# Summing both halves of a modulation vector over partitions in one group of products

## The chip, the cores and the metric

One core of a Trainium2 chip runs one program. The metric is the device time of one execution in microseconds, as the median over several runs of the same program on the same chip.

## What is computed

Two layers of a conditioned decoder trunk, all in f32, with 256 rows of 1024 columns. Each layer is a feed-forward block, a token mixer and another feed-forward block. Each of the three gets a shift, a scale and a gate, which are nine vectors of 1024 numbers computed from a condition vector `c`:

```python
c_act = jax.nn.silu(c)
for l in range(DEPTH):
    mod = c_act @ w_ada[l] + b_ada[l]
    sh1, sc1, g1, sh2, sc2, g2, sh3, sc3, g3 = jnp.split(mod, N_MOD, axis=-1)
    x = x + 0.5 * g1[:, None, :] * swiglu(modulate(x, sh1, sc1), ffn1_gate[l], ffn1_up[l], ffn1_down[l])
    x = x + g2[:, None, :] * token_mix(modulate(x, sh2, sc2), ...)
    x = x + 0.5 * g3[:, None, :] * swiglu(modulate(x, sh3, sc3), ffn2_gate[l], ffn2_up[l], ffn2_down[l])
return rms_norm(x) * final_norm
```

`modulate` is an RMS norm, times 1 + scale, plus shift. `swiglu(u)` is `(silu(u @ w_gate) * (u @ w_up)) @ w_down` with 2816 hidden columns. What the token mixer does inside does not matter here.

## The kernel before, in words

**Products.** An f32 product is made from three products of a faster format: a weight block is split into a high part (`whi`, a copy by ACT, L177) and a low part (`wlo`, the rest, by DVE, L179), the other operand likewise (`uhi` and `ulo`, or `hh` and `hl` for the hidden tile), and high times high, low times high and high times low are added up in PSUM. One split makes a unit of 128x1024. Weight blocks of 1 MB arrive by DMA from SP's queue in a pool `raws` of four buffers (tile name `raw`), two units to a block. A buffer is free again when its last reader is done, and only then can the DMA of the next block that was given that buffer go out.

**Feed-forward block (`ffn`).** For each of the groups of 256 hidden columns a gate block and an up block are loaded (L625, L626), each gives two units, and `ws_tile` makes 24 products of 256 columns for each unit; `finish_tile` makes the hidden tile from them (`sg` by ACT, `hf32` by DVE, L494, `hh` by ACT, `hl` by DVE, L496). Then the down matrix comes in two column halves (c = 0 and 1), in blocks of four 128-row tiles (L432), two units to a block, twelve products of 512 columns to a unit.

**The modulation vectors (`ada_half`).** They are computed beside this, in pieces: one half of a vector, 512 columns of `w_ada`, is two blocks (L216) of 128x4x512. For each block DVE makes four multiply-and-add instructions into an accumulator `acc` of 128x512 (L222; each takes one of eight columns of `c_act`, `cact`), so that what is left is a sum over the 128 partitions, which `finish` does on PE. A *row channel* (2, 5, 8: the gates) starts from the bias (`binit`), is split by ACT (L229) and DVE (L230) into a high and a low tile, and `finish` sums each with one product of 512 columns against a block of ones, so that the sum stands in every partition. A *column channel* (0, 1, 3, 4, 6, 7: shifts and scales) is wanted with its numbers along the partitions: `column_sums` makes four f32 products of 128 columns whose stationary operand is 32 columns of ones, one for each strip of 32 rows of PSUM; `pick_columns` multiplies by a mask (`mcol`, L194) and reduces (`cs`, L197), and `add_bias` makes the columns (`col`, L203). Channels of layer 0's first block are made otherwise, in `begin`, which uses `pick_columns` too.

All accumulators, of row and of column channels, come from one pool, `keep`, tag `acc`, with two buffers. An accumulator is free again when its products (column) or its two splits (row) are done.

**Order.** `ada_load` takes a list of halves and makes a generator. Each `ada_step`, which `ffn` calls at a group of hidden columns (one or two steps) and at each block of the down matrix (one), brings one w_ada block; a `finish` is issued at the step after its half is complete. The lists are: first feed-forward block of either layer: channels 2, 3, 4, 5, 6 of that layer, two halves each; token mixer of layer 0: channel 7; second feed-forward block of layer 0: channel 8, then 1, 0, 7 of layer 1; token mixer and second block of layer 1: none and channel 8. So ten column vectors go through `ada_half`, in the order 3, 4, 6, 7 of layer 0, and 1, 0, 7, 3, 4, 6 of layer 1. The order of instructions within each engine, and which buffer of a pool a tile gets, are set by a scheduler when the kernel is built, not by hand (save in `begin`).

Of the kernel before, what the change touches and what calls it, by code (L numbers as in the profile page):

```python
# [10 lines left out]
F32 = mybir.dt.float32  # L11
F32R = mybir.dt.float32r
AF = mybir.ActivationFunctionType
ALU = mybir.AluOpType
AX = mybir.AxisListType

P = 128
D = 1024
KD = D // P
# [58 lines left out]
def hybrid_trunk(ctx, tc, t, out):  # L78
    nc = tc.nc
# [7 lines left out]
    keep = ctx.enter_context(tc.tile_pool(name="keep", bufs=1))  # L87
    scr = ctx.enter_context(tc.tile_pool(name="scr", bufs=2))
    small = ctx.enter_context(tc.tile_pool(name="small", bufs=4))
# [14 lines left out]
    def mm(o, a, b, start, stop):  # L104
        last_mm[0] = nc.tensor.matmul(o, a, b, start=start, stop=stop)  # L105
# [7 lines left out]
    ones = const.tile([P, P], F32R, name="ones")  # L113
# [12 lines left out]
    colmask = tab[:, TAB_COL:TAB_COL + 32]  # L126
# [14 lines left out]
    def pool_unit(pool):  # L141
        return (pool.tile([P, 1024], F32R, name="whi", tag="whi"),
                pool.tile([P, 1024], F32R, name="wlo", tag="wlo"))
# [39 lines left out]

    mods = {}

    def column_sums(ps, vec, a, start, stop):

        av = a.rearrange("p (j i r) -> p j i r", j=4, i=4)
        for i in range(4):
            mm(ps[32 * i:32 * i + 32, :P].rearrange("p (j r) -> p j r", j=4), vec, av[:, :, i, :], start, stop)  # L190

    def pick_columns(ps):
        m = small.tile([P, 4, 32], F32, name="mcol", tag="mcol", bufs=1)
        nc.vector.tensor_tensor(m, ps[:, :P].rearrange("p (j r) -> p j r", j=4),  # L194
                                colmask[:, None, :].to_broadcast([P, 4, 32]), ALU.mult)
        cs = small.tile([P, 4], F32, name="cs", tag="cs", bufs=2)
        nc.vector.tensor_reduce(cs, m, AX.X, ALU.add)  # L197
        return cs

    def add_bias(l, ch, n, cs):  # L200
        if (l, ch) not in mods:
            mods[l, ch] = small.tile([P, KD], F32, name="col", tag="col", bufs=8)
        nc.vector.scalar_tensor_tensor(mods[l, ch][:, n * 4:n * 4 + 4], cs, 1.0 if ch in (1, 4, 7) else 0.0,  # L203
                                       bcols[:, l, ch * 8 + n * 4:ch * 8 + n * 4 + 4], ALU.add, ALU.add)

    def ada_half(l, ch, n):
        acc = keep.tile([P, 512], F32, name="acc", tag="acc", bufs=2)
        row = ch in (2, 5, 8)
        n0 = ch * D + n * 512
        wv = t["w_ada"][l].rearrange("(p j) n -> p j n", p=P)  # L210
        if row:
            nc.scalar.dma_start(binit[0:1, :], t["b_ada"][l:l + 1, n0:n0 + 512])
        for j in range(0, KD, 4):
            r = raw_tile()
            rv = r.rearrange("p (j n) -> p j n", j=4)
            nc.sync.dma_start(rv, wv[:, j:j + 4, n0:n0 + 512])  # L216
            for jj in range(4):
                cj = cact[:, j + jj:j + jj + 1]
                if j + jj == 0 and not row:
                    nc.vector.tensor_scalar_mul(acc, rv[:, jj, :], cj)  # L220
                else:
                    nc.vector.scalar_tensor_tensor(acc, rv[:, jj, :], cj, binit if j + jj == 0 else acc,  # L222
                                                   ALU.mult, ALU.add)
            yield
        if row:
            if n == 0:
                mods[l, ch] = keep.tile([P, D], F32, name="g", tag="g", bufs=2)
            hi, lo = (scr.tile([P, 512], F32R, name="acc%d" % i, tag="uf", bufs=2) for i in range(2))
            nc.scalar.activation(hi, acc, AF.Copy)  # L229
            nc.vector.tensor_tensor(lo, acc, hi.bitcast(F32), ALU.subtract)  # L230

            def finish():
                ps = trps()
                mm(ps, ones, hi, True, False)
                mm(ps, ones, lo, False, True)
                nc.scalar.activation(mods[l, ch][:, n * 512:(n + 1) * 512], ps, AF.Copy, scale=1.0 if ch == 5 else 0.5)
        else:
            def finish():
                ps = trps()
                column_sums(ps, ones[:, :32].bitcast(F32), acc, True, True)  # L240
                cs = pick_columns(ps)
                add_bias(l, ch, n, cs)
        ada_late.append(finish)

    ada_late = []
# [211 lines left out]
    def ffn(l, which, uhi, ulo, ada_plan, post, xn=None, side=None):  # L457
# [4 lines left out]
        with tc.tile_pool(name="ffn", bufs=1) as fp, tc.tile_pool(name="fu", bufs=EXTRA) as fu, \  # L462
# [5 lines left out]
            unit_kinds[:] = ["w"] * 4 + ["f"] * EXTRA  # L468
            unit_count[0] = 0
            unit_alloc["f"] = lambda: pool_unit(fu)  # L470
            bank_pools[:] = [psum, fps]
            ada_load(ada_plan)

# [24 lines left out]
            def begin():  # L498
# [7 lines left out]
                ada, gu, more, accs, sums, units = {}, {}, {}, {}, {}, {}  # L506
# [35 lines left out]
                    accs[q] = acc  # L542

                def operands(q):
                    cs = pick_columns(sums[q])
                    for i, ch in enumerate((1, 0)):
                        nc.vector.scalar_tensor_tensor(mods[l, ch][:, q * 2:q * 2 + 2], cs[:, i * 2:i * 2 + 2], float(ch),
                                                       bcols[:, l, ch * 8 + q * 2:ch * 8 + q * 2 + 2], ALU.add, ALU.add)
# [70 lines left out]
            for grp in range(2 if xn is None else 3, KF // 2):  # L619
# [8 lines left out]
                for i in range(2):  # L628
                    f = grp * 2 + i
                    ps = mmps()  # L630
# [13 lines left out]
                xs_gemm(units, ktiles(h[0]), ktiles(h[1]), 512, evac, 6 if c else 0, last if c else None)  # L644
            unit_kinds[:] = ["w"]
            bank_pools[:] = [psum]


    def token_mix(l, uhi, ulo, ada_plan, post):
# [459 lines left out]
    bcols = const.tile([P, DEPTH, 72], F32, name="bcols")  # L1109
# [36 lines left out]
    for hf in range(NH):  # L1146
        r, a, _ = half_rstd(hf)
# [59 lines left out]
```

## Time and profile before

| | |
|---|---|
| median of 3 runs | 1188.9 us (1186.39 to 1190.99) |
| profiled execution | 1184.94 us |
| its span | 1183.1 us |
| mean granted clock of TensorE | 0.995 |
| PE busy | 1151.3 us, 97% of the span |
| DVE busy | 939.1 us, 79% |
| ACT busy | 642.6 us, 54% |

PE is TensorE, DVE VectorE, ACT ScalarE, and SP the engine whose queue issues the weight DMAs. Products are pipelined on PE, so rows of single products overlap, and their distance from start to start is what they cost. Busy shares are means over stages with different limits; the stage that matters here is layer 1's first feed-forward block, whose down products begin at 731 us. L105 is the helper that issues every product, so products are told apart by their tiles: `mm` is a weight product, `tr<-acc,ones` the sum over partitions of an accumulator.

### The profile page before, as it was taken

What the parts mean: (1) busy time and instruction counts of PE and PEld (TensorE: products, weight loads), DVE (VectorE), ACT (ScalarE), POOL (GpSimd) and SP (SyncE); (2) the same over time, 40 slices, a digit from 0 to 9 for tenths busy, and PEclk for the clock granted to TensorE, in tenths of its full rate; (3) what the DMA queues carried; (4) which work ended last, traced back from release to release, by engine and by line L of the source; (5) the groups of instructions that cost most, each with busy time, mean ns of one, the idle gap of its engine ahead of it and who ended that gap; (6) DMA issues with size and microseconds to landing.
All of it is one profiled execution on the core that took longest, in us unless ns stands there. A gap on an engine that the chain in (4) does not pass through costs nothing.

```text
span 1183.1 us, 20211 instructions
## 1 busy us (share of the span) xinstructions
PE 1151.3 (97%) x7886; PEld 1011.7 (86%) x7886; DVE 939.1 (79%) x1889; ACT 642.6 (54%) x1156; POOL 2.2 (0%) x13
## 2 busy tenths in 40 slices
PE   4999999999999999999999999999999999999997
PEld 3799988789977889998879999888997788999985
DVE  4999998778888898798488879975878888865553
ACT  4545444647676564544465444465676756554441
POOL 0000000000000000000000000000000000000000
PEclk8999999999999999999999999999999999999999
DMA  9989999595623579898739979965664264985540
GB/s 331 337 289 342 333 347 364 163 266 168 178 96 104 192 228 306 286 324 311 254 110 312 317 258 349 338 232 146 178 204 117 72 200 133 306 258 189 181 140 36
DMA packets 201970, 274.95 MB, mean 232 GB/s; under 512 B 13613, under 2 KB 119815, under 8 KB 201875
## 3 DMA queue, kind: packets, MB, share of 16 engines
q1 hardware_dynamic: 201119, 273.02, 70.5%
q8 instruction: 62, 1.02, 0.4%
q10 hardware_dynamic: 756, 0.64, 0.2%
q14 instruction: 33, 0.27, 0.1%
HBM read 272.60 MB, written 1.05 MB: 231 GB/s over the span
## 4 chain that ended last, share of the span: by engine, by line
PE 86%; DVE 7%; DMA 3%; ACT 2%; issue 1%; SPq 1%; DVEq 0%; ACTq 0%
PE mm L105 77%; PE tr L108 3%; DMA raw<-in_w_ada 2%; PE sc L105 2%; PE po L105 2%; DVE wlo L179 2%; PE tr L105 2%; ACT whi L177 1%; DVE win L723 1%; DVE acc L222 0%; DVE kd L745 0%; DMA c_in<-in_c 0%; ACT junk L293 0%; DVE acc L541 0%; DVE x L453 0%
## 5 line engine op out<-in xcount | busy, mean ns | idle before, releaser
L179 DVE TENSOR_TENSOR wlo<-raw,whi 128x1024 fp32r<-128x1024 f32 (+5 forms) x400 | 423.0, 1073 | 120.1 <-ACT whi L177 119.3
L177 ACT ACTIVATE whi<-raw 128x1024 fp32r<-128x1024 f32 (+5 forms) x400 | 364.3, 936 | 232.2 <-PE mm L105 103.0
L105 PE MATMUL mm<-uhi,whi 128*128 128x256 f32 x1248 | 348.4, 279 | 0.0
L105 PE MATMUL mm<-uhi,wlo 128*128 128x256 f32 x1248 | 347.1, 278 | 0.0
L105 PE MATMUL mm<-ulo,whi 128*128 128x256 f32 x1248 | 347.1, 278 | 0.0
L105 PEld LDWEIGHTS mm<-ulo,whi 128*128 128x128 f32 x1248 | 236.2, 189 | 0.5
L105 PEld LDWEIGHTS mm<-uhi,whi 128*128 128x128 f32 x1248 | 234.2, 188 | 2.5 <-issue 1.4
L105 PEld LDWEIGHTS mm<-uhi,wlo 128*128 128x128 f32 x1248 | 234.4, 188 | 0.0
L222 DVE SCALAR_TENSOR_TENSOR acc<-raw,cact,acc 128x512 f32<-128x512 f32 x224 | 167.0, 747 | 5.4 <-DMA raw<-in_w_ada 2.4
L105 PE MATMUL mm<-whi,hh 128*128 128x512 f32 x352 | 138.3, 393 | 0.0
L105 PE MATMUL mm<-whi,hl 128*128 128x512 f32 x352 | 137.1, 390 | 0.0
L105 PE MATMUL mm<-wlo,hh 128*128 128x512 f32 x352 | 137.0, 389 | 0.0
L105 PE MATMUL mm<-whi,uhi 128*128 128x512 f32 (+3 forms) x336 | 126.7, 379 | 4.9 <-ACT uhi L554 3.5
L105 PE MATMUL mm<-whi,ulo 128*128 128x512 f32 (+3 forms) x336 | 126.9, 378 | 1.4 <-DVE ulo L342 1.4
L105 PE MATMUL mm<-wlo,uhi 128*128 128x512 f32 (+3 forms) x336 | 125.7, 374 | 0.0
L495 ACT ACTIVATE hh<-hf 128x256 fp32r<-128x256 f32 x70 | 29.1, 416 | 99.3 <-DVE hf L494 99.3
L105 PEld LDWEIGHTS mm<-whi,hh 128*128 128x128 f32 x352 | 66.1, 188 | 15.1 <-issue 1.4
L105 PEld LDWEIGHTS mm<-whi,hl 128*128 128x128 f32 x352 | 66.1, 188 | 13.9
L105 PEld LDWEIGHTS mm<-whi,uhi 128*128 128x128 f32 x336 | 63.5, 190 | 16.8 <-ACT uhi L554 4.1
L105 PEld LDWEIGHTS mm<-wlo,hh 128*128 128x128 f32 x352 | 66.1, 188 | 13.3
L105 PEld LDWEIGHTS mm<-whi,ulo 128*128 128x128 f32 x336 | 63.9, 190 | 12.0 <-DVE ulo L342 3.1
L105 PEld LDWEIGHTS mm<-wlo,uhi 128*128 128x128 f32 x336 | 63.8, 190 | 9.4 <-DVE wlo L179 0.2
(245 smaller groups left out, 1325.3 us busy)
## 6 DMA issues: line engine op xcount, KB each, us to landing
raw<-in_w_ada SPq DMA_DIRECT2D x72, 1024.0 KB, 7.9
raw<-in_ffn_gate SPq DMA_DIRECT2D x41, 1024.0 KB, 7.0
raw<-in_ffn_up SPq DMA_DIRECT2D x41, 1024.0 KB, 6.8
raw<-in_ffn_down SPq DMA_DIRECT2D x40, 1024.0 KB, 7.9
raw<-in_w_in SPq DMA_DIRECT2D x18, 1024.0 KB, 6.8
raw<-in_w_in SPq DMA_DIRECT2D x16, 512.0 KB, 6.2
raw<-in_w_out SPq DMA_DIRECT2D x8, 1024.0 KB, 5.1
raw<-in_ffn_down SPq DMA_DIRECT2D x8, 512.0 KB
```

The source lines that it names most:

```text
L105: last_mm[0] = nc.tensor.matmul(o, a, b, start=start, stop=stop)
L108: nc.tensor.transpose(o, a, ident)
L177: nc.scalar.activation(a, s, AF.Copy)
L179: nc.vector.tensor_tensor(b, s, a.bitcast(F32), ALU.subtract)
L222: nc.vector.scalar_tensor_tensor(acc, rv[:, jj, :], cj, binit if j + jj == 0 else acc, ALU.mult, ALU.add)
L495: nc.scalar.activation(h[0][:, f, :], hf32, AF.Copy)
L723: nc.vector.tensor_tensor(win[i][jj * 64:(jj + 1) * 64, 8 * a:8 * a + 8, g, :], pv[g * 64:(g + 1) * 64, jj, :, a:a + 15], cols[0][jj * 64: ...
```

## The change

The two halves of a column vector are kept in two accumulators (`held`) until the second is complete. Then one `finish` makes 8 products into 128x256 of PSUM, one multiplication, one reduction and one bias for all eight columns. A count of the vectors (`pairs`) sends those with an even number, while a feed-forward block runs, to two accumulators of that block's pool (tag `sgx`, `acc_rooms`); odd ones, and those outside, take the two of `keep`, as row channels do. By that count the vectors of layer 0 are 1 (channel 3, `keep`), 2 (4, `sgx`), 3 (6, `keep`), 4 (7, `keep`, in the token mixer), and those of layer 1 are 5 (1, `keep`), 6 (0, `sgx`), 7 (7, `keep`), 8 (3, `sgx`), 9 (4, `keep`), 10 (6, `sgx`).

```diff
--- before.py
+++ after.py
@@ -183,29 +183,35 @@
 
     mods = {}
 
-    def column_sums(ps, vec, a, start, stop):
-
-        av = a.rearrange("p (j i r) -> p j i r", j=4, i=4)
-        for i in range(4):
-            mm(ps[32 * i:32 * i + 32, :P].rearrange("p (j r) -> p j r", j=4), vec, av[:, :, i, :], start, stop)
-
-    def pick_columns(ps):
-        m = small.tile([P, 4, 32], F32, name="mcol", tag="mcol", bufs=1)
-        nc.vector.tensor_tensor(m, ps[:, :P].rearrange("p (j r) -> p j r", j=4),
-                                colmask[:, None, :].to_broadcast([P, 4, 32]), ALU.mult)
-        cs = small.tile([P, 4], F32, name="cs", tag="cs", bufs=2)
-        nc.vector.tensor_reduce(cs, m, AX.X, ALU.add)
+    def column_sums(ps, vec, halves):
+
+        for n, a in enumerate(halves):
+            av = a.rearrange("p (j i r) -> p j i r", j=4, i=4)
+            for i in range(4):
+                mm(ps[32 * i:32 * i + 32, n * P:(n + 1) * P].rearrange("p (j r) -> p j r", j=4), vec, av[:, :, i, :],
+                   True, True)
+
+    def pick_columns(ps, n):
+        m = small.tile([P, KD, 32], F32, name="mcol", tag="mcol", bufs=1)
+        nc.vector.tensor_tensor(m[:, :n], ps[:, :n * 32].rearrange("p (j r) -> p j r", j=n),
+                                colmask[:, None, :].to_broadcast([P, n, 32]), ALU.mult)
+        cs = small.tile([P, KD], F32, name="cs", tag="cs", bufs=2)
+        nc.vector.tensor_reduce(cs[:, :n], m[:, :n], AX.X, ALU.add)
         return cs
 
-    def add_bias(l, ch, n, cs):
-        if (l, ch) not in mods:
-            mods[l, ch] = small.tile([P, KD], F32, name="col", tag="col", bufs=8)
-        nc.vector.scalar_tensor_tensor(mods[l, ch][:, n * 4:n * 4 + 4], cs, 1.0 if ch in (1, 4, 7) else 0.0,
-                                       bcols[:, l, ch * 8 + n * 4:ch * 8 + n * 4 + 4], ALU.add, ALU.add)
+
+    acc_rooms = [None]
+    pairs = [0]
+    held = []
 
     def ada_half(l, ch, n):
-        acc = keep.tile([P, 512], F32, name="acc", tag="acc", bufs=2)
         row = ch in (2, 5, 8)
+        if not row and n == 0:
+            pairs[0] += 1
+        if not row and pairs[0] % 2 == 0 and acc_rooms[0] is not None:
+            acc = acc_rooms[0]()
+        else:
+            acc = keep.tile([P, 512], F32, name="acc", tag="acc", bufs=2)
         n0 = ch * D + n * 512
         wv = t["w_ada"][l].rearrange("(p j) n -> p j n", p=P)
         if row:
@@ -235,11 +241,19 @@
                 mm(ps, ones, lo, False, True)
                 nc.scalar.activation(mods[l, ch][:, n * 512:(n + 1) * 512], ps, AF.Copy, scale=1.0 if ch == 5 else 0.5)
         else:
+            held.append(acc)
+            if n == 0:
+                return
+            halves = list(held)
+            held.clear()
+
             def finish():
                 ps = trps()
-                column_sums(ps, ones[:, :32].bitcast(F32), acc, True, True)
-                cs = pick_columns(ps)
-                add_bias(l, ch, n, cs)
+                column_sums(ps, ones[:, :32].bitcast(F32), halves)
+                cs = pick_columns(ps, KD)
+                mods[l, ch] = small.tile([P, KD], F32, name="col", tag="col", bufs=8)
+                nc.vector.scalar_tensor_tensor(mods[l, ch], cs, 1.0 if ch in (1, 4, 7) else 0.0,
+                                               bcols[:, l, ch * 8:ch * 8 + 8], ALU.add, ALU.add)
         ada_late.append(finish)
 
     ada_late = []
@@ -468,6 +482,7 @@
             unit_kinds[:] = ["w"] * 4 + ["f"] * EXTRA
             unit_count[0] = 0
             unit_alloc["f"] = lambda: pool_unit(fu)
+            acc_rooms[0] = lambda: fp.tile([P, 512], F32, name="acc", tag="sgx", bufs=2)
             bank_pools[:] = [psum, fps]
             ada_load(ada_plan)
 
@@ -542,7 +557,7 @@
                     accs[q] = acc
 
                 def operands(q):
-                    cs = pick_columns(sums[q])
+                    cs = pick_columns(sums[q], 4)
                     for i, ch in enumerate((1, 0)):
                         nc.vector.scalar_tensor_tensor(mods[l, ch][:, q * 2:q * 2 + 2], cs[:, i * 2:i * 2 + 2], float(ch),
                                                        bcols[:, l, ch * 8 + q * 2:ch * 8 + q * 2 + 2], ALU.add, ALU.add)
@@ -644,6 +659,7 @@
                 xs_gemm(units, ktiles(h[0]), ktiles(h[1]), 512, evac, 6 if c else 0, last if c else None)
             unit_kinds[:] = ["w"]
             bank_pools[:] = [psum]
+            acc_rooms[0] = None
 
 
     def token_mix(l, uhi, ulo, ada_plan, post):
```

On DVE, in layer 1's first feed-forward block, where the additions of row channel 5's first half begin. Before, its accumulator is `acc_8116`, made from the w_ada blocks `raw_8118` and `raw_8264`; `raw_8113` is an up block and `raw_8252` the first down block:

```order
L179 TENSOR_TENSOR wlo_8217<-raw_8113,whi_8216 128x1024 [waits PE_49,Activation_49]
L222 SCALAR_TENSOR_TENSOR acc_8116<-raw_8118,cact_89,binit_87 128x512 [waits DMAHW6_49]
L494 TENSOR_TENSOR hf32_8045<-mm_7986,sg_8043 128x256 [waits Activation_49]
L222 SCALAR_TENSOR_TENSOR acc_8116<-raw_8118,cact_89,acc_8116 128x512 [waits DVE_49] x2
L496 TENSOR_TENSOR hl_6758<-hf32_8045,hh_6757 128x256 [waits Activation_49]
L222 SCALAR_TENSOR_TENSOR acc_8116<-raw_8118,cact_89,acc_8116 128x512 [waits DVE_49]
L179 TENSOR_TENSOR wlo_8271<-raw_8252,whi_8270 128x1024 [waits DMAHW7_49,Activation_49]
L179 TENSOR_TENSOR wlo_8287<-raw_8252,whi_8286 128x1024 [waits PE_49,Activation_49]
L222 SCALAR_TENSOR_TENSOR acc_8116<-raw_8264,cact_89,acc_8116 128x512 [waits DMAHW0_49,DVE_49]
```

After, the accumulator is `acc_8057`, from `raw_8059` and `raw_8210`; `raw_8295` is the third down block, `mcol_8204`, `cs_8206` and `col_8208` belong to the column vector before it (channel 4), and `acc_8255` to row channel 5's second half:

```order
L179 TENSOR_TENSOR wlo_8308<-raw_8295,whi_8307 128x1024 [waits DMAHW3_49,Activation_49]
L228 SCALAR_TENSOR_TENSOR acc_8057<-raw_8059,cact_89,binit_87 128x512 [waits DMAHW6_49,PE_49]
L509 TENSOR_TENSOR hf32_8187<-mm_8128,sg_8185 128x256 [waits Activation_49]
L228 SCALAR_TENSOR_TENSOR acc_8057<-raw_8059,cact_89,acc_8057 128x512 [waits DVE_49]
L196 TENSOR_TENSOR mcol_8204<-tr_8195,tab_85 128x256 [waits PE_49]
L228 SCALAR_TENSOR_TENSOR acc_8057<-raw_8059,cact_89,acc_8057 128x512 [waits DVE_49]
L511 TENSOR_TENSOR hl_6716<-hf32_8187,hh_6715 128x256 [waits Activation_49]
L228 SCALAR_TENSOR_TENSOR acc_8057<-raw_8059,cact_89,acc_8057 128x512 [waits DVE_49]
L199 TENSOR_REDUCE cs_8206<-mcol_8204 128x8
L228 SCALAR_TENSOR_TENSOR acc_8057<-raw_8210,cact_89,acc_8057 128x512 [waits DMAHW0_49,DVE_49]
L255 SCALAR_TENSOR_TENSOR col_8208<-cs_8206,bcols_100 128x8 [waits DVE_49]
L228 SCALAR_TENSOR_TENSOR acc_8255<-raw_8257,cact_89,binit_87 128x512 [waits DMAHW4_49,DMAHW2_49]
```

The first addition stood directly behind the last up split and waited for a DMA; it now stands behind the split of the third down block and waits for PE too. The additions of the second half (`acc_8255`) are interleaved with those of the first.

On PE, at the end of the up products of the same block. Before:

```order
L105 MATMUL mm_8187<-ulo_6661,whi_8216 128x256
L105 MATMUL mm_8187<-uhi_6660,wlo_8217 128x256
L105 MATMUL tr_8254<-acc_7962,ones_81 32x128 [waits PE_49]
L105 MATMUL tr_8254<-acc_7962,ones_81 32x128 x3
L105 MATMUL mm_8250<-whi_8270,hh_6757 128x512 [waits Activation_49]
```

After:

```order
L105 MATMUL mm_8128<-ulo_6619,whi_8157 128x256
L105 MATMUL mm_8128<-uhi_6618,wlo_8158 128x256
L105 MATMUL tr_8195<-acc_7626,ones_81 32x128 x4
L105 MATMUL tr_8195<-acc_7914,ones_81 32x128 x4
L105 MATMUL mm_8191<-whi_8216,hh_6715 128x512 [waits Activation_49]
```

The group between the last up product and the first down product has eight products, from two accumulators, where it had four from one.

On PE, four down units later, where the sums of row channel 5's first half stand (`acc0` and `acc1` are its high and low tiles). Before:

```order
L105 MATMUL mm_8251<-wlo_8334,hh_6757 128x512
L105 MATMUL mm_8251<-whi_8333,hl_6758 128x512
L105 MATMUL tr_8351<-acc0_8305,ones_81 128x512 [waits PE_49]
L105 MATMUL tr_8351<-acc1_8306,ones_81 128x512
L105 MATMUL mm_8250<-whi_8361,hh_6757 128x512 [waits Activation_49]
```

After:

```order
L105 MATMUL mm_8192<-wlo_8280,hh_6715 128x512
L105 MATMUL mm_8192<-whi_8279,hl_6716 128x512
L105 MATMUL tr_8297<-acc0_8251,ones_81 128x512 [waits PE_49,Activation_49]
L105 MATMUL mm_8191<-whi_8307,hh_6715 128x512
L105 MATMUL mm_8191<-wlo_8308,hh_6715 128x512 [waits DVE_49]
L105 MATMUL tr_8297<-acc1_8252,ones_81 128x512 [waits DVE_49]
```

The sums stand at the same place of the stream, and each has gained a wait of its own, the first for ACT, the second for DVE.

## Rows read from the trace of the kernel before

**Rows 1.** Page: busy us of each engine; the chain that ended last, by engine.
```profile
PE 1151.3 (97%) x7886; PEld 1011.7 (86%) x7886; DVE 939.1 (79%) x1889; ACT 642.6 (54%) x1156; POOL 2.2 (0%) x13
...
PE 86%; DVE 7%; DMA 3%; ACT 2%; issue 1%; SPq 1%; DVEq 0%; ACTq 0%
```

**Rows 2.** Windows view, four stretches; columns as in its first line.
```profile
core 0: us, PE busy (x) PEld busy (x) DVE busy (x) ACT busy (x) POOL busy (x), PEclk, DMA share, GB/s
14.80:18.50 3.70, 0.29 (x3) 0.05 (x1) 2.87 (x7) 2.03 (x3) 0.00 (x0) 0.83 1.10 349
17.30:24.10 6.80, 5.48 (x16) 3.91 (x20) 4.28 (x8) 1.78 (x3) 0.00 (x0) 0.50 1.08 351
220.00:310.00 90.00, 85.88 (x642) 78.33 (x641) 75.87 (x172) 57.95 (x122) 0.31 (x1) 1.00 0.76 221
731.00:757.00 26.00, 26.00 (x122) 21.35 (x122) 25.64 (x36) 11.36 (x16) 0.00 (x0) 1.00 0.99 345
```

**Rows 3.** PE's timeline around 731 us and at 742 us: start, us, line, operation, xcount.
```profile
730.69 0.28 PE L105 MATMUL mm<-ulo,whi 128*128 128x256 f32 x1
730.80 0.28 PE L105 MATMUL mm<-uhi,wlo 128*128 128x256 f32 x1
731.00 0.43 PE L105 MATMUL tr<-acc,ones 128*32 128x128 f32 x8
731.36 0.50 PE L105 MATMUL mm<-whi,hh 128*128 128x512 f32 x1
731.70 0.39 PE L105 MATMUL mm<-wlo,hh 128*128 128x512 f32 x1
731.93 0.40 PE L105 MATMUL mm<-whi,hl 128*128 128x512 f32 x1
...
742.38 0.62 PE L105 MATMUL tr<-acc,ones 128*128 128x512 f32 x2
```

**Rows 4.** Chain of waits, in order of time: start, us, what.
```profile
35.43 1.03 PE tr L105 x64
...
731.43 11.11 PE mm L105 x48
```

**Rows 5.** Groups by tile: ns min/median/max, first and last start, forms.
```profile
L194 DVE TENSOR_TENSOR mcol<-tr,tab x24: 278/282/291, 16.6 to 774.0; 128x128 f32<-128x128 f32 x24
L197 DVE TENSOR_REDUCE cs<-mcol x24: 273/278/289, 16.9 to 776.0; 128x4 f32<-128x128 f32 x24
L203 DVE SCALAR_TENSOR_TENSOR col<-cs,bcols x20: 149/155/166, 114.7 to 777.3; 128x4 f32<-128x4 f32 x20
```

**Rows 6.** DVE's timeline around 721 us and at 733 us: start, us.
```profile
720.85 2.35 DVE L179 TENSOR_TENSOR wlo<-raw,whi 128x1024 fp32r<-128x1024 f32 x2
723.12 0.74 DVE L222 SCALAR_TENSOR_TENSOR acc<-raw,cact,binit 128x512 f32<-128x512 f32 x1
723.78 0.42 DVE L494 TENSOR_TENSOR hf<-mm,sg 128x256 f32<-128x256 f32 x1
724.12 1.53 DVE L222 SCALAR_TENSOR_TENSOR acc<-raw,cact,acc 128x512 f32<-128x512 f32 x2
...
733.41 0.68 DVE L230 TENSOR_TENSOR acc<-acc,acc 128x512 fp32r<-128x512 f32 x1
```

**Rows 7.** SP's queue, 709 to 729 us: issues of weight blocks.
```profile
709.62 0.37 SPq L625 DMA_DIRECT2D raw<-in_ffn_gate  x1
...
723.23 0.37 SPq L432 DMA_DIRECT2D raw<-in_ffn_down  x1
...
728.94 0.37 SPq L432 DMA_DIRECT2D raw<-in_ffn_down  x1
```

**Rows 8.** ACT's timeline, 715 to 737 us; in brackets the idle time before.
```profile
715.15 2.01 ACT L177 ACTIVATE whi<-raw 128x1024 fp32r<-128x1024 f32 x2 [2.58 <-DMA raw<-in_ffn_gate]
...
730.27 1.04 ACT L177 ACTIVATE whi<-raw 128x1024 fp32r<-128x1024 f32 x1
732.39 0.64 ACT L229 ACTIVATE acc<-acc 128x512 fp32r<-128x512 f32 x1 [1.08 <-DVE acc L222]
...
736.91 2.01 ACT L177 ACTIVATE whi<-raw 128x1024 fp32r<-128x1024 f32 x2 [0.89 <-DMA raw<-in_ffn_down]
```

## The prediction

> **What bounds the kernel now.** The page's busy shares come first: PE 97% of the span of 1183.1 us, DVE 79%, and the chain that ended last lies 86% on PE [rows 1]. Time is therefore won only by taking work off PE or by closing a hole in PE's stream, and it is lost wherever something makes PE wait. The windows come next, to see which engine stands close behind PE. In layer 1's first feed-forward block, in the 26 us where its down products begin, PE is busy all 26.00 us but DVE 25.64 and the DMA share is 0.99 [rows 2]: three resources are full at once, so an order in which one of them is asked late has no slack to hide in. In the token mix of layer 0 (220 to 310 us) PE is busy 85.88 of 90.00. The same view tells one thing about PE's clock: after the stretch 14.80 to 18.50, in which PE had 0.29 us of work, the granted clock is 0.50 in 17.30 to 24.10, that is the lower level, 1.2 GHz instead of 2.4; before 14.80 and in the later windows it is 1.00.
>
> **The products, -3.0 us.** The change issues the same number of products in ten groups of 8 instead of twenty of 4. What a group of 4 costs PE: products of 256 columns start .11 apart and products of 512 columns .23 apart (731.70 to 731.93), so from the product at 730.80 to the second 512-wide one at 731.70 there would be .34 us without the group, and there are .90 [rows 3]. The group costs .56. What the second four cost behind the first four is not shown directly; the nearest row is a long stream of the same 32-column products, 64 records of 64 columns in 1.03 us [rows 4]. The 8 records of 128 columns that one half makes [rows 3] are then 8 x 1.03 / 64 x 2 = .26. So a vector costs .56 + .26 instead of 2 x .56: .30 less, ten times, **-3.0**. The bounds are 0 (the second half costs all of .56 again) and -5.6 (it costs nothing, which the stream in rows 4 excludes). I take the stream, because it is the same kind of product without a change of kind between.
>
> The Trainium skill bears on this in two places. "FP8 and Floating Point Precision", section "TensorE Precision Notes", says that true FP32 takes 4 passes through the array; "TensorE: Matmul & The Clock Gate", "Part 3: Packing small matmuls", says that products in different column tiles run side by side. An estimate by the first alone, the strips one after another, is 4 products x 4 passes x 128 columns at 2.4 GHz = .85 for a half, and the change would gain nothing here; by both it is .21, and this term -3.5. The measured .56 for a whole group [rows 3] is less than .85 and so bears out the two together.
>
> **The vector work, 0.** Before, each half has a multiplication of .28, a reduction of .28 and a bias of .155 [rows 5], 1.43 for two halves. After, one of each at twice the width: the width at most doubles the work, so 1.43 is the upper bound and .72 the lower. Between nothing and 7 us over the kernel leave DVE. It comes off DVE while PE is the full one [rows 2], so I cost it at 0; without that cover it would be a gain of at most .7 for each vector.
>
> **The held accumulators, +8.6 us.** This is the term that decides. The two new buffers go to even-numbered vectors only. In layer 0 the vector before row channel 5 (channel 4) is the second, so it has the new buffers. Layer 1 starts one count later, and there channel 4 is the ninth: it holds both `keep` buffers until its group of 8 has run, and row channel 5, next in line, needs one of them. In the order of before, row channel 5's first addition waits for its DMA alone; in that of after also for PE, that is for the group which now stands between the last up tile and the first down product, at 731.0 [rows 3]. Before, those additions began at 723.12 [rows 6]. A wait of 8 us on an addition is not yet a wait of PE; what hangs on it is the following.
>
> Row channel 5's accumulation holds two of the four `raw` buffers until its additions are done. In the built kernel a third goes to the next w_ada block, so the two next blocks of the down matrix must share the fourth. The second of them cannot be asked for before the first is split, and the DVE order puts the split of the second ahead of the delayed additions. I follow the chain: the up block's last split ends at 723.1 (the pair at 720.85 [rows 6]), and the down block goes out at 723.23 as now [rows 7]. It is used at 730.27 now [rows 8], which I keep. Two ACT splits (2.01 [rows 8]) and behind them the second DVE split (2.35 a pair, so 1.2) end at 733.5; the DMA of the next block goes out then, not at 728.94 [rows 7]. Landing took 8.0 from 728.94 to 736.91, with other blocks in flight, and 5.5 from 709.62 to 715.15 [rows 7, 8]; less is in flight now, so 5.5: 739.0. An ACT split (1.0) and a DVE split (1.2) follow: 741.2. Only then DVE comes to the additions: before row 5's accumulator is complete the order has 8 of its own and 3 of the next one, .66 each (723.12 to 723.78 [rows 6]), 7.3, with hf and hl (.34 each, 723.78 to 724.12) and the three instructions of the column vector (at most 1.4) between: 750.6. ACT's copy takes .64 [rows 8]: 751.2. On PE the sum over partitions of that copy stands behind four down units, now at 742.38 [rows 3]; the chain of waits has 11.11 us of products there [rows 4], and with the group's .26 PE comes to it at 742.6. PE waits 8.6 us. The bounds: every landing at the quick 5.5 makes the chain about 4 earlier, so 4.4; the landing of 8.0 for the second block makes it 2.5 later, so 11. I take **7.5**, a little below the chain, since three waits in it may overlap in part.
>
> The low part of the sum stands two products behind, and waits for a DVE split of the next unit (1.2) and its own subtraction of .68 [rows 6], after the last of the foreign additions (.66): 2.5 behind the last own addition, against .64 + about .7 for what PE does meanwhile: **+1.1** (0 to 1.5).
>
> A PE that has stood for 7.5 us is likely to get the lower clock, as after the 3.4 idle us at 14.80: 6.8 us at 0.50, of which 1.2 lay in the idle stretch itself [rows 2], so 5.6 us at half speed lose **2.8** (0 to 3.4). The later down blocks come late too, but while PE runs at half speed they catch up; I cost that at 0, and at up to 3 if the clock stays.
>
> **What else moves, 0.** In layer 0's token mix the channel 7 vector's three DVE instructions and its group move behind the second half. PE idles 4.1 us in those 90 us [rows 2], so the move may cost or give about as much at the most; with no wait that clearly hangs on it I take 0. Layer 1's token mix keeps its order, and SP issues the same DMAs in the same order.
>
> **Sum.** -3.0 + 7.5 + 1.1 + 2.8 = +8.4. The profiled execution of 1184.94 us becomes 1193.3. It lies 4.0 under the median of the three runs, 1188.9, so the median becomes **1197.3**. A measurement of this kernel can tell about 0.5%, 5.9 us, from no change: below 1183.0 is faster, above 1194.8 slower.
>
> **Rivals.**
> *The wait without the clock* (0.15): PE waits but keeps 1.00. Speaks for it that PE had been full for hundreds of us, which it had not before 14.80. Then the late blocks cost something instead, about 1.5: +7.1, 1196.0.
> *A short wait* (0.18): the landings take 5.5 each, since fewer blocks are in flight, and the chain comes 4 earlier: wait 4.0, low part 1.1, no fall of the clock: +2.1, 1191.0. Against it stands the DMA share of 0.99 [rows 2].
> *The chain is hidden* (0.09): not slower. It decides at one point: if the second down block were asked for by about 725, the additions would be done before PE comes to the sum at 742.6. The place is the order in which the `raw` buffers come free; if the copies were released earlier than I read, only the products' gain is left: -3.0, 1185.9. Against it: two buffers held and one taken leave one for two blocks.
> *The group of 8 gains nothing* (0.08): each half costs its .56 as before, because the strips or the halves are not streamed (the strips in turn, as the first of the two pages alone would have it). Then the change does on PE nothing of what it says, and only the waits remain: +11.4, 1200.3.
> The forecast itself has 0.50.
>
> **Range and chances.** The forecast's own bounds, 4.4 to 11 for the wait and 0 to 3.4 for the clock, give 1192 to 1202. The range goes from 1188.5, which takes in the short wait, to 1203.5 for no gain on the groups with a long wait; left out are the hidden chain and the tails. Slower: of the forecast 0.44, without the clock 0.12, short wait 0.03, no gain 0.08, together 0.67. Faster: only a hidden chain with luck in the token mix, 0.04. The rest, 0.29, is within 0.5%.
>
> **What would show it.** In the changed kernel the group of 8 takes about .8 where .56 stood. A hole of PE of 5 to 9 us lies near 742 to 751 before the sum of a 512-wide accumulator, released by ACT's copy and behind it by DVE's additions, and the second down block is issued near 733 instead of 729. After the hole the granted clock is 0.50 for some us. Wrong would be the forecast if PE is busy without a break from 731 to 757, or if the hole is there and the additions stand ahead of the second block's split. If the time comes out right but the loss lies in layer 0's token mix, the reason was wrong.

## The result, and the profile after

The changed kernel takes 1195.31 us (median of 6 runs, 1194.33 to 1200.58), the kernel before 1187.66 beside it (6 runs). The ratio is 1.0068, with a 95% interval of 1.0053 to 1.0083: 8.1 us slower (7.7 between the two medians), where 8.4 had been forecast. The profiled execution of the changed kernel, 1200.58 us, is the longest of its six, so its rows tell where the time goes and not, to a microsecond, how much. The page of the changed kernel, its busy times and the chain by engine:

```profile
PE 1157.1 (97%) x7886; PEld 1017.8 (85%) x7886; DVE 938.0 (78%) x1859; ACT 642.0 (54%) x1156; POOL 2.2 (0%) x13
...
PE 65%; DVE 16%; DMA 12%; ACT 4%; issue 3%; SPq 1%; DVEq 0%; ACTq 0%
```

In the chain PE fell from 86% [rows 1] to 65%, and DVE and DMA took its place. That alone is no measure of waiting: PE is busy for 97% of the span as before, and the chain runs through DVE and DMA also where PE had no wait. The waits of PE between 700 and 800 us tell where it stood (us in total, times, longest):

```profile
PE tr L105 <- ACT acc L235: 6.4, 1, 6.4
PE mm L105 <- DVE ss L309: 1.4, 1, 1.4
```

The windows view of the changed kernel, with the columns of [rows 2]:

```profile
731.00:757.00 26.00, 19.51 (x108) 15.71 (x107) 17.64 (x28) 6.62 (x10) 0.00 (x0) 0.85 0.49 166
```

Before, PE was busy all 26.00 us of that stretch, DVE 25.64, and the DMA share was 0.99 [rows 2]. Now PE has 19.51, the granted clock is 0.85 and the DMA share has halved: all three stand still in turn. PE's timeline in it:

```profile
734.97 0.64 PE L105 MATMUL tr<-acc,ones 128*32 128x128 f32 x16
735.55 0.50 PE L105 MATMUL mm<-whi,hh 128*128 128x512 f32 x1
...
746.35 0.39 PE L105 MATMUL mm<-whi,hl 128*128 128x512 f32 x1
753.14 0.80 PE L105 MATMUL tr<-acc,ones 128*128 128x512 f32 x1 [6.40 <-ACT acc L235]
753.74 0.63 PE L105 MATMUL mm<-whi,hh 128*128 128x512 f32 x1
754.16 0.63 PE L105 MATMUL mm<-wlo,hh 128*128 128x512 f32 x1
754.88 0.80 PE L105 MATMUL tr<-acc,ones 128*128 128x512 f32 x1
...
758.89 0.63 PE L105 MATMUL mm<-wlo,hh 128*128 128x512 f32 x1
759.32 0.51 PE L105 MATMUL mm<-whi,hl 128*128 128x512 f32 x1
759.66 0.40 PE L105 MATMUL mm<-whi,hh 128*128 128x512 f32 x1
```

The group of 8 takes .58 to the next start, where the group of 4 took .36 [rows 3]. Twelve us behind it PE waits 6.40 us for ACT's copy of row channel 5's accumulator, and behind the wait the products start .43 apart instead of .23 until 759.3. What stood before the copy is in DVE's timeline, and below it in SP's queue:

```profile
733.80 2.36 DVE L179 TENSOR_TENSOR wlo<-raw,whi 128x1024 fp32r<-128x1024 f32 x2 [2.70 <-ACT whi L177]
...
742.51 1.23 DVE L179 TENSOR_TENSOR wlo<-raw,whi 128x1024 fp32r<-128x1024 f32 x1 [5.11 <-ACT whi L177]
743.66 0.75 DVE L228 SCALAR_TENSOR_TENSOR acc<-raw,cact,binit 128x512 f32<-128x512 f32 x1
```

```profile
724.46 0.37 SPq L446 DMA_DIRECT2D raw<-in_ffn_down  x1
...
736.18 0.37 SPq L446 DMA_DIRECT2D raw<-in_ffn_down  x1
```

The first addition starts at 743.66, 8.7 us after the group it was held for, because the third down block was asked for only at 736.18, when the second was split, and DVE splits the third ahead of the additions.

### The profile page after: what moved, and what is told of

It is laid out like the page before. It is cut to its first block, busy times and chain, and to the rows that moved or that the text cites. A ratio compares the mean times of both kernels' runs of the same rounds, so it can differ in the third digit from the quotient of the medians.

```text
span 1198.8 us, 20178 instructions
## 1 busy us (share of the span) xinstructions
PE 1157.1 (97%) x7886; PEld 1017.8 (85%) x7886; DVE 938.0 (78%) x1859; ACT 642.0 (54%) x1156; POOL 2.2 (0%) x13
## 4 chain that ended last, share of the span: by engine, by line
PE 65%; DVE 16%; DMA 12%; ACT 4%; issue 3%; SPq 1%; DVEq 0%; ACTq 0%
PE mm L105 56%; DVE wlo L179 7%; DMA raw<-in_ffn_up 5%; DMA raw<-in_w_ada 4%; DVE acc L228 3%; PE tr L108 3%; ACT whi L177 2%; PE sc L105 2%; PE po L105 2%; PE tr L105 1%; DMA raw<-in_ffn_down 1%; DMA raw<-in_ffn_gate 1%; DVE win L739 1%; DVE rtmp L466 0%; DVE hf L509 0%
```

## The experiments

Twelve kernels ran, each beside runs of the kernel before on the same chip, where its median was 1188.9 to 1189.3.

**1. The conflict taken away by the count.**

```diff
-        if not row and n == 0:
+        if not row and n == 0 and acc_rooms[0] is not None:
             pairs[0] += 1
```

> The vector of the token mixer is no longer counted, so in both layers the vector ahead of row channel 5 (channel 4) gets the new accumulators and nothing else changes. Theory A (row channel 5 waits for a held accumulator, and the order behind it stops PE): the first addition of row channel 5 in layer 1 waits for its DMA alone again, PE has no hole between 731 and 757 us, the clock stays at 1.00 there, and only the gain of the groups is left: 574 ns for 8 products against 2 x 356, and one change of kind less, .34 a vector, so 1187.7 - 3.4 = 1184.3, ratio 0.997. Theory B (the loss sits in the held groups or in layer 0's token mixer, and the hole in layer 1 is a disturbance): the time stays at 1192 to 1197.

Ratio 0.9989 (0.9977 to 1.0002), median 1188.44. The first addition starts at 721.26 again and PE has no hole:

```profile
731.00:757.00 26.00, 26.00 (x136) 21.56 (x135) 25.33 (x37) 11.43 (x16) 0.00 (x0) 1.00 0.97 340
```

One line that only changes which buffers a vector gets brings back about 9 us (1.0068 against 0.9989). Theory B is out. But the time is 1.3 below the kernel before and not 3.4, and the interval takes in no gain at all; that is taken up in experiments 6, 7, 11 and 12.

**2. The conflict taken away by the list.** In layer 1 the first block's list becomes

```diff
-HALVES(l, 2, 3, 4, 5, 6)
+HALVES(l, 2, 3, 4, 5, 6) if l == 0 else HALVES(l, 2, 5, 3, 4, 6)
```

> In layer 1 the list of the first feed-forward block is channels 2, 5, 3, 4, 6 instead of 2, 3, 4, 5, 6. The vector before a row channel no longer holds both buffers of the pool, though the count, the rooms and the groups are the changed kernel's. Theory A: no hole of PE over 1 us in that block, 1184 to 1187. Theory B: 1192 to 1197, since the groups and the token mixer are the same.

Ratio 1.0004 (0.9989 to 1.0018); PE is busy all 26.00 us from 731 to 757 and there is no hole. The median of 1189.54 is above the range given, and like the kernel before. Two edits with nothing in common but that row channel 5 meets a free buffer remove the loss.

**3. The additions first on DVE.** The buffer is still held; only the split of the third down block is ordered behind the additions.

```diff
-                    nc.vector.scalar_tensor_tensor(acc, rv[:, jj, :], cj, binit if j + jj == 0 else acc,
+                    i = nc.vector.scalar_tensor_tensor(acc, rv[:, jj, :], cj, binit if j + jj == 0 else acc,
...
+                    if (l, ch, n, j + jj) == (1, 5, 0, KD - 1):
+                        hold(4, "dve", i)
```

> The accumulator is still held and the first addition still waits for PE, but the split of the third down block's first unit is ordered on DVE behind row channel 5's last addition. Theory A in its narrow form (the order on DVE behind the wait makes the hole): the additions start when the group of 8 is done, at about 735 us, 8.9 us later the copy is made, and PE, which comes to the sum some 12 us behind the group, waits 2 us or less: 1185 to 1189. Theory A in its wide form (the buffer's wait alone is enough): the hole stays at 5 us or more, 1193 to 1196.

Ratio 1.0059 (1.0040 to 1.0079): nothing gained that the intervals can tell, and PE waits 5.33 and .94. But it isn't the buffer alone either. DVE's and then ACT's timeline:

```profile
737.09 0.75 DVE L228 SCALAR_TENSOR_TENSOR acc<-raw,cact,binit 128x512 f32<-128x512 f32 x1
743.24 0.42 DVE L511 TENSOR_TENSOR hf<-mm,sg 128x256 f32<-128x256 f32 x1 [5.40 <-ACT sg L509]
```

```profile
740.93 1.06 ACT L177 ACTIVATE whi<-raw 128x1024 fp32r<-128x1024 f32 x1 [4.21 <-DMA raw<-in_ffn_down]
...
742.85 0.36 ACT L509 ACTIVATE sg<-mm 128x256 f32<-128x256 f32 x1
```

The first addition runs at 737.09 as wanted. The second stands behind `hf` of the last hidden tile, `hf` waits for ACT's silu, and the silu stands on ACT behind the split of the same late block. The block holds up the additions by two routes.

**4. Both routes closed.** Besides the edit of experiment 3, that split goes behind the accumulator's copy on ACT.

```diff
-            nc.scalar.activation(hi, acc, AF.Copy)
+            i = nc.scalar.activation(hi, acc, AF.Copy)
+            if (l, ch, n) == (1, 5, 0):
+                hold(2, "act", i)
```

> As the run with the additions first on DVE, and in addition ACT makes the split of the third down block behind the copy of row channel 5's accumulator, so that the last hidden tile's silu, for which DVE's next instruction waits, no longer stands behind that block's DMA. Theory A in its narrow form, for both engines: the additions run from 737 to 746, PE waits at most 3 us in all at the sums and the next unit, the clock does not fall for long: 1187 to 1190. Theory A in its wide form (buffer alone): hole of 5 us or more, 1193 to 1196.

Ratio 1.0014 (1.0001 to 1.0027), 1190.66: 6 us of the 8 come back though the buffer is held as long; the median lies .7 above the range that was given for both orders. In its profile the additions run from 737.47, the copy is made at 746.28, and the sums find it done:

```profile
748.59 0.62 PE L105 MATMUL tr<-acc,ones 128*128 128x512 f32 x2
...
770.03 0.73 PE L105 MATMUL mm<-whi,hh 128*128 128x512 f32 x2 [0.83 <-ACT whi L177]
771.88 0.50 PE L105 MATMUL mm<-wlo,hh 128*128 128x512 f32 x1 [1.11 <-DVE ss L313]
```

What is left are short waits for later blocks. So the held accumulator opens the hole, and the order behind it on two engines gives it its size.

**5. Held, but two groups of 4.** `finish` loops over the two halves and makes group, multiplication, reduction and bias for each.

```diff
-                column_sums(ps, ones[:, :32].bitcast(F32), halves)
+                for i, a in enumerate(halves):
+                    ps = trps()
+                    column_sums(ps, ones[:, :32].bitcast(F32), [a])
...
```

> Accumulators are held and given out as in the changed kernel, but each half has its own group of 4 products, multiplication, reduction and bias again, both after the second half. Theory A: the hole is there as in the changed kernel, 5 to 7 us with the clock at 0.50 behind it, and the gain of the groups is gone: 1195.3 + 3.4 = 1198.7. Theory C (the group of 8 and its wide vector instructions make the hole): no hole, 1187 to 1189.

Ratio 1.0049 (1.0031 to 1.0068). The hole is there (3.28 and then 1.24 us in the profiled execution, shorter than the 5 to 7 expected), which rules theory C out. That the gain would be gone was wrong, and PE's timeline says why:

```profile
731.33 0.65 PE L105 MATMUL tr<-acc,ones 128*32 128x128 f32 x16
731.90 0.50 PE L105 MATMUL mm<-whi,hh 128*128 128x512 f32 x1
```

The scheduler put the two groups next to each other, and PE pays .57 for both, as for the group of 8. It is the neighbourhood of the products that saves, not that they are one group.

**6. Groups in the feed-forward blocks only.** Experiment 1, with channel 7 of layer 0, in the token mixer, left as it was before.

```diff
-            held.append(acc)
-            if n == 0:
-                return
-            halves = list(held)
+            together = acc_rooms[0] is not None
+            if together:
+                held.append(acc)
+                if n == 0:
+                    return
+            halves = list(held) if together else [acc]
...
```

> As the run that counts vectors inside the feed-forward blocks only, but channel 7 of layer 0, which runs in the token mixer, keeps its two groups of 4 as before; PE's order in that token mixer is then that of the kernel before. Theory D (the token mixer's new order of products costs about 2.3 us between 276 and 290 us, and each of the nine other groups gains .34): 9 x .34 = 3.1 below the kernel before, 1185.8, ratio 0.9974, and the lag against the kernel before stays level through 276 to 290 us. Theory E (the groups gain less than .34): ratio 0.999, as the run with the token mixer's vector grouped too.

Ratio 0.9982 (0.9971 to 0.9993), 1186.36: 2.1 us faster than the kernel before (0.8 to 3.4), between the two theories.

**7. Group in the token mixer only.** The same condition turned round, and no new accumulators.

```diff
+            together = acc_rooms[0] is None
...
```

> The opposite: the kernel before, with only channel 7 of layer 0, in the token mixer, held and summed in one group of 8. Theory D: the new order costs 2.3, the group gives .34: 1190.9, ratio 1.0016. Theory E: no loss there, ratio 0.9997.

Ratio 1.0000 (0.9985 to 1.0015). By time neither theory is excluded, since 1.8 us either way lie in the interval. PE's timeline tells them apart: from the first product behind the token mixer's last group to its first product with the tile `sc`, in the kernel before and then here:

```profile
261.37 0.38 PE L105 MATMUL mm<-uhi,whi 128*128 128x256 f32 x1
...
309.69 0.29 PE L105 MATMUL sc<-kc,qs 128*128 128x32 f32 x2
```

```profile
262.54 0.39 PE L105 MATMUL mm<-uhi,whi 128*128 128x256 f32 x1
...
312.22 0.29 PE L105 MATMUL sc<-kc,qs 128*128 128x32 f32 x2
```

That is 48.32 us before and 49.68 here. In all nine profiled executions with a group of 8 in the token mixer it is 49.64 to 49.76, in the four that keep two groups apart there 48.32 to 48.35 (experiment 6 among them), and with the two groups of experiment 5 48.91. So theory D is right in kind: the order that comes with the group there costs 1.36 us, not 2.3, against the .34 that the group saves. Which wait in that stretch makes it was not followed up.

**8. The hole filled.**

```diff
+                if (l, ch, n) == (1, 5, 0):
+                    for _ in range(28):
+                        mm(ps.rearrange("p (a b) -> p a b", a=4), ones, ones[:, None, :].to_broadcast([P, 4, P]), True, True)
                 mm(ps, ones, hi, True, False)
```

> The changed kernel with 28 products of 512 columns of ones (6.4 us) put on PE ahead of the sum that waits in layer 1; their results are overwritten. Theory F (the lower clock behind the hole costs 3 us of its own): PE has no hole over 1.5 us there, the clock stays at 1.00 in 750 to 760 us, and the time falls by about 3 to 1192.3. Theory G (what limits PE behind the hole is the late blocks, so the clock costs nothing): 1195 to 1196, with new waits of PE in place of the slow products.

Ratio 1.0068 (1.0053 to 1.0084), as the changed kernel, though in the profiled execution the clock stays up:

```profile
745.00:750.00 5.00, 5.00 (x24) 4.11 (x23) 5.00 (x9) 0.63 (x1) 0.00 (x0) 1.00 0.64 210
750.00:755.00 5.00, 5.00 (x24) 4.11 (x23) 4.33 (x6) 0.91 (x1) 0.00 (x0) 1.00 0.98 338
755.00:760.00 5.00, 5.00 (x24) 4.15 (x23) 4.78 (x6) 2.59 (x5) 0.00 (x0) 1.00 1.05 388
```

In that execution ACT's copy started at 749.05 and took .63, while the 28 products lasted until 751.9: they filled 2.3 us more than the hole was long, about what the clock can have given. So it doesn't settle what the clock costs.

**9. Half filled.** Half as many products.

```diff
-                    for _ in range(28):
+                    for _ in range(14):
```

> As the run with the filled hole, with 14 products of ones (3.2 us) instead of 28, less than the hole was in any run so far. Theory F (the lower clock costs time of its own): the granted clock behind the hole stays at 1.00 and the time falls by about 2, ratio 1.005. Theory G: ratio 1.0068 as the changed kernel.

Ratio 1.0065 (1.0043 to 1.0086), inconclusive too. PE still waited 2.72 us behind the 14 products and .94 at the low part's sum, and the clock fell all the same:

```profile
750.00:755.00 5.00, 4.05 (x10) 2.87 (x10) 4.22 (x6) 0.60 (x1) 0.00 (x0) 0.50 0.97 328
```

**10. The conflict moved to layer 0.**

```diff
-    pairs = [0]
+    pairs = [1]
```

> The count starts at one, so odd and even change places: now layer 0's channel 4 holds both buffers of the pool ahead of row channel 5, and layer 1's has the new ones. Theory A: the hole moves with it: PE waits 3 to 7 us at the sum of row channel 5 in layer 0, some 12 us behind the first down product (about 173 us), and layer 1 has none; ratio 1.004 to 1.008. Theory H (layer 1's place is special): no hole in either layer, ratio 0.999.

Ratio 1.0041 (1.0022 to 1.0061). Layer 1's hole is gone (PE 25.00 of 25.00 from 735 to 760), and layer 0 has got waits, but short ones. PE's waits from 155 to 215 us, and then the clock:

```profile
PE mm L105 <- DVE wlo L179: 1.7, 1, 1.7
PE tr L105 <- DVE acc L236: 0.5, 1, 0.5
```

```profile
190.00:200.00 10.00, 8.45 (x30) 6.79 (x31) 9.89 (x15) 4.83 (x9) 0.00 (x0) 0.83 0.99 344
```

In layer 0 the third down block had been split by 161.4, before the group at 161.86, and DVE ran the additions from 162.35 on, as soon as the accumulator was free. The loss moved with the conflict, which bears out theory A, but the hole of 3 to 7 us was wrong: without a late block in the way the same conflict costs less.

**11 and 12. The slow step.** Reading why experiments 1 and 6 gave less than their groups, I found that runs of products of 256 columns come at two steps (last section), and tried to switch the step with an added group of 4.

```diff
+                if n == 1 and (l, ch) in ((0, 8), (1, 2), (1, 8)):
+                    column_sums(trps(), ones[:, :32].bitcast(F32), [tab[:, :512]])
```

> The run with groups in the feed-forward blocks only, and an added group of 4 products (on a constant table, its result unused) behind the second row sum of channel 8 of layer 0, 2 and 8 of layer 1. Theory I (products of 256 columns stand in stretches at 117.8 or 113.3 ns; a row sum puts PE to the slow step, the next group of 32-column products back to the fast one): from 474 to 508, 665 to 699 and 1048 to 1113 us the step is 113.3, which gives 3.8% of 34.5 + 34.5 + 65 = 5.1 for 3 x 0.58 = 1.7: 3.4 faster than that run, ratio 0.9954 against the kernel before. Theory J (the step is set by something else, such as what DVE does at the time): the step stays 117.8 and the time rises by 1.7, ratio 0.9997.

> The kernel before with the same three added groups. Theory I: the slow stretches to the next group are 473 to 495, 664 to 686 and 1048 to 1113 us there: 3.8% of 22 + 22 + 65 = 4.1 gained for 1.7: ratio 0.998. Theory J: 1.7 slower, ratio 1.0015.

On the kernel of experiment 6 the ratio to the kernel before is 0.9976 (0.9959 to 0.9994), median 1185.70, the lowest of all, where theory I gave 0.9954; on the kernel before it is 0.9985 (0.9966 to 1.0005). Against experiment 6 itself that is less than the intervals can tell, though the step did change. The chain of waits of experiment 6, and then of experiment 11 (start, us, what):

```profile
474.56 33.92 PE mm L105 x288
508.48 0.57 PE tr L105 x16
```

```profile
475.58 32.84 PE mm L105 x288
508.42 0.57 PE tr L105 x16
```

The same 288 products take 1.08 us less behind the added group, which itself costs .36 in the chain. Theory J, that the step would stay, is out. But the 288 products behind the group of 8 at 508 then ran at the slow step, 118 ns, where in experiment 6 they ran at 113, and that took back more than had been gained; it went the same way in layer 1's first block. Only the third added group, with no group of 8 behind it, kept its gain.

## Why the prediction was right, and where it was not

**The direction, the place and the size** came from the step that read the order: row channel 5's first addition had gained a wait for PE, and the third down block's split stood ahead of it. Experiments 1 and 2 show that the conflict is the cause of the loss, 10 that it moves with the conflict, 3 and 4 show the order behind it. The profiled execution is 15.7 us longer in span than that of before. By the starts of the same weight products in both, 11.6 of these come between 731 and 770 us of the kernel before, the forecast place, and 3.0 in layer 0's token mixer, the place that the prediction had named as a sign of a wrong reason. They are not the bulk, but the term for it was wrong (below).

**The wait, 7.5.** The hole was 6.40 in this execution, and 5.33 and 3.28 in experiments 3 and 5: it depends on how long the blocks take. The chain was as written, link by link: second block asked for at 724.46 (reckoned 723.23), third at 736.18 (733.5), addition at 743.66 (741.2), sum at 753.14 (751.2). It came 1 to 3 us later than reckoned, and PE itself 4.0 later (734.97 against 731.00 at the group [rows 3]), so the wait is shorter than the 8.6 of the chain. The lower bound of 4.4 does not follow from its reason: of the two landings in the chain one was already reckoned at the quick 5.5, and the other, at most 7.0 (723.23 to 730.27), could make it 1.5 earlier, not 4. The low side of the range and the rival of the short wait rest on the same 4. One link was missing: I named DVE's order alone, and experiment 3 showed that ACT's order holds the same additions by a second route.

**The low part, 1.1, and the clock, 2.8.** From 753.14 to 759.32 PE makes 13 steps; at .23 each they would take 3.0 us, and they took 6.2. So both terms together cost 3.2, where 3.9 had been forecast. The halved clock (.43 a step) makes 2.6 of it, near the forecast. The steps behind the two row sums, .60 instead of .43, make .3, and the low part's sum makes the last .3: it starts at 754.88, .72 behind the product ahead of it. That is 1.74 behind the high part's sum, as in experiments 3, 5 and 9, where no product lies between the two and PE waits .94, 1.24 and .94; here two products at half speed cover most of it. The prediction added the two terms as if they did not overlap. By time the clock's cost was not shown, since neither filled kernel came out faster; it is read from rows only.

**The groups, -3.0.** One group of 8 behind a product of 256 columns costs .22 more than a group of 4 (.58 against .36 to the next start). That is nearer to the .21 that the estimate from the two pages of the Trainium skill gave ("FP8 and Floating Point Precision", "TensorE Precision Notes", and "TensorE: Matmul & The Clock Gate", "Part 3: Packing small matmuls") than to the .26 from [rows 4]; the row had been the upper one of two close values. By it .34 a vector is saved, 3.4 in all. But the kernels without the hole gained 1.3 (experiment 1) and 2.1 (experiment 6). **This is the step that failed**: it priced the products taken away, and not what their absence does to the products around them. In the kernel before, the first group of the second feed-forward block of layer 0 stood at 495.04 and ended a slow stretch; in the changed kernel the vector's only group stands at 511.36, and the slow stretch lasts until there:

```profile
472.43 22.61 PE mm L105 x192
495.04 0.36 PE tr L105 x8
495.40 11.10 PE mm L105 x96
```

```profile
477.44 33.92 PE mm L105 x288
511.36 0.57 PE tr L105 x16
```

In the first, of the kernel before, 192 products take 117.8 ns each and then 96 take 115.6, with the group's edge in it; in the second, of the changed kernel, all 288 take 117.8. That is 96 products more at a step that is 4.5 ns longer, .4 us, and the same again in layer 1's first block. In layer 0's first block the changed kernel's 192 products between the group at 132.43 and the down products were slow too, .9 us, where those of before were fast. Together 1.7 of the 3.4 are given back in this execution. The share differs between executions: layer 0's first block starts at the fast step in these two and at the slow one in those of experiments 1 and 6, so the 1.3 and 2.1 are not a sum of such rows.

**The vector work, 0:** the wide instructions take .42, .41 and .16 where two sets took 1.43 [rows 5], .44 off DVE for each vector, and PE shows nothing of it. That lay inside the bounds and under the cover named.

**What else moves, 0.** This failed too. The token mixer's new order costs 1.3 to 1.4 us in every profiled execution that has it (experiment 7), which takes back another part of the 3.4. The rest of the 3.0 lost there in the changed kernel's execution came with a granted clock of 0.89 and 0.94 in 250 to 260 and 260 to 270 us. The execution of experiment 12 has 0.94 and 0.88 there with the token mixer of the kernel before, so that is not the change's doing. The later wait of 1.40 us at 779.05 (released by DVE) belongs to the late blocks, which were costed at 0 if the clock falls and at up to 3 if it stays; it fell, and they cost 1.40 all the same.

That the sum met the result to within a microsecond is partly luck: the hole was 1.1 shorter and the low part and the clock cost .7 less than forecast, and against that the later wait, the slow step and the token mixer's order cost what had been put at 0.

## What to carry to other kernels

A buffer that is held until its partner is done makes the next user of its pool wait for everything up to that point: count, over the whole program, who is next after each holder, since an alternation that is right in one layer can be off by one in the next. Then follow the wait through the in-order queues of every engine: what it costs is decided by what stands ahead of and behind the waiting instruction, here the split of a block that could not yet be loaded. A count that runs on only where the two rooms exist (experiment 1), with the group left out of the token mixer (experiment 6), keeps the idea and is 2.1 us faster than the kernel before. And a gain of tenths of a microsecond for each group is easily lost to a new order elsewhere, so compare the start of the same product in both traces, stage by stage.

## What the runs showed of the hardware that was not expected

Products of 256 columns in the same loop, with PE busy and the granted clock at 1.00, come in stretches at 117.8 or at 113.3 ns from start to start. The stretches change at the sums over partitions. In the 14 profiled executions of this study, wherever there were enough such products on both sides to tell: the first row sum of a row channel (layer 0's 8, layer 1's 2 and 8) turned a fast stretch into a slow one 41 times of 41, and the second left the step slow (36 of 36, where no added group followed). That does not hold in layer 0's first block, where the second row sum of channel 2 turned slow into fast 10 times, fast into slow twice, and left it slow twice. A group of 4 was followed by the fast step every time, 23 times from the fast and 10 from the slow (6 of these directly behind a row sum, the added groups); a group of 8 changed the step every time, 23 times to the fast and 9 times to the slow. What sets the step was not found. The slow one costs 3.8% of such a stretch, so a group's place and its number of products count for more here than its own .2 us.

The granted clock fell towards its lower level behind waits of PE of 6.40, 3.28 and 2.72 us (0.50, 0.72 and 0.50 in the windows behind them), the last directly behind 3.4 us of products that served only to keep PE busy. Shorter waits went either way: behind 1.80 us at 255 in the changed kernel's token mixer it fell (0.94 in 260 to 270), behind 2.19 us at the same place in experiment 10's it stayed at 1.00.
